# One transfer of dense expert weights for eight blocks into one buffer, in place of four blocks into each of two

## The chip, the cores and the metric

The kernel runs on one core of one Trainium2 chip. The metric is the device time of one execution in microseconds, the median of the runs. The core has five engines that run side by side and each take their instructions strictly in the order of the program: TensorE (PE; its weight loads are PEld), VectorE (DVE), ScalarE (ACT), GpSimd (POOL) and SyncE (SP, which here issues nearly all plain DMAs). The tile framework adds the semaphore waits, and its scheduler, which plays the program through against a model, fixes the order on each engine when the program is built.

## The reference, cut to what matters

An encoder layer for 1024 tokens of width 1024 ends in a PEER feed-forward: each token picks 8 x 16 of 16384 experts and sums their outputs.

```python
def chunk(xc):
    q = (xc @ w_q).reshape(C, PEER_HEADS, 2, PEER_DK // 2)
    s = jnp.einsum('chpd,hpnd->chpn', q, sub_keys)
    ...
    g = jax.nn.softmax(best, axis=-1)
    u = u_tab[eidx]
    a = jax.nn.gelu(jnp.einsum('chkd,cd->chk', u, xc), approximate=False)
    vv = v_tab[eidx]
    return jnp.einsum('chk,chkd->cd', (g * a).astype(vv.dtype), vv)
```

## The kernel before

The PEER part treats the eight tiles of 128 tokens in two ways. Three tiles (`NG`) go through `gather`: for each of 128 picks POOL fetches one row of `peer_u` or `peer_v` per token by an indirect DMA (L1249, tile `grow`), and DVE takes a dot product with it (L1262) or adds it to `gacc` (L1270). These DMAs run in a queue of POOL's own. Five tiles (`DENSE`, 640 tokens) are computed densely over all 16384 experts, in 128 blocks of 128 experts:

- `u_part(i)` (U): 48 matmuls of 320 columns give the activations `A` (128 experts x 640 tokens) of block i, with Gelu on ACT (L1221). 72 blocks (`EARLY`) are done ahead and parked in DRAM (`a_d`); the other 56 are done in the last stage.
- `build_g` has written the dense gate weights to DRAM as `g_d`, token slice by token slice: 20 slices of 32 tokens, each 128 x 128 x 32. For one block a partition's piece in one slice is 32 floats, and neighbouring blocks lie side by side.
- `weigh(i)` multiplies `A` by the block's gate weights `gt` on DVE (L1372) and splits the product into `wh` and `wl` (L291 on ACT, L292 on DVE). The first block of each four (`GI`) issues the DMA that loads `gt` for the four (L1368). `gt` has two buffers, so a load waits until the last multiply that reads the four before the last four is done.
- `v_group` (V) takes eight weighed blocks (`GRP`), in two halves of 512 columns. For each block it loads `vr` from `peer_v` (L1392, three buffers), splits it into `vh` (ACT, L291) and `vl` (DVE, L292; four buffers each), and runs 15 matmuls of 512 columns into five accumulators, which DVE then adds to `f_sb` (L1409).

The last stage consists of 16 such groups; 9 use parked blocks and 7 compute theirs. SP issues `vr`, `A`, `ur` (for U) and `gt` in one queue, in the order that the scheduler gave them: a `vr` that stands behind a `gt` is issued behind it and moves behind it. DVE mixes the work of the dense part with that of `gather`, ACT does the `vh`, `wh` and `uh` casts and the Gelu. `A` has three buffers, `wh` and `wl` eight each.

Of the kernel before, what the change touches and what calls it, by code (L numbers as in the profile page):

```python
# [10 lines left out]
F32 = mybir.dt.float32  # L11
# [10 lines left out]
P = 128  # L22
# [11 lines left out]
GRP = 8  # L34
# [255 lines left out]
def split(nc, hi, lo, src):  # L290
    nc.scalar.copy(hi, src)  # L291
    return nc.vector.tensor_sub(lo, src, hi)  # L292
# [3 lines left out]
def layer(ctx: ExitStack, tc: tile.TileContext, a: dict, out: bass.AP):  # L296
# [835 lines left out]


    CS = 32
    GI = 4
    NCS = TD // CS
    jx_d = dram.tile([NT, 3, P, P], BF16, name="jx_d")
    NB = 4
# [219 lines left out]
    ep = s_e.enter_context(tc.tile_pool(name="ep", bufs=2, side="left"))  # L1358
# [3 lines left out]
    def weigh(i, A):  # L1362
        if A is None:
            A = up.tile([P, TD], F32, name="A", bufs=3)
            nc.sync.dma_start(A, a_d[i])
        if i % GI == 0:
            gt = ep.tile([P, NCS, GI, CS], F32, name="gt")
            nc.sync.dma_start(gt, h_view[:, :, i:i + GI, :])  # L1368
            G[i // GI] = gt
        gt = G[i // GI]  # L1370
        Av = A.rearrange("p (s c) -> p s c", c=CS)
        nc.vector.tensor_mul(Av, Av, gt[:, :, i % GI])  # L1372
        wh = ep.tile([P, TD], F32R, name="wh", bufs=GRP)
        wl = ep.tile([P, TD], F32R, name="wl", bufs=GRP)
        split(nc, wh, wl, A)
        return wh, wl
# [85 lines left out]
    for n, g in enumerate(order):  # L1462
        W, As = [], {}

        def first_half(b):
            if g >= n_e:
                As[b] = u_part(g * GRP + b, u_late)
                tick(UC)

        if n == 0:  # L1470
            for b in range(3):
                first_half(b)
        with ExitStack() as s_i:
            if n == 0:
                s_i.enter_context(tc.issue_after(loads[-1].ins))
            for c in range(DENSE if n == 0 else 0):
                nc.sync.dma_start(f_sb[:, c], h2_d[NG + c])
            for b in range(GRP):
                if b not in As:
                    first_half(b)  # L1480
                W.append(weigh(g * GRP + b, As.get(b)))
            if n == n_g - 1:
                load_last_ln()
            v_group(g * GRP, W, n == 0, n == n_g - 1)
# [70 lines left out]
```

## Time and profile before

| what | value |
|---|---|
| median of 3 runs | 3265.74 us (3262.74 to 3266.41) |
| the profiled execution | 3255.75 us, its span 3254.0 us |
| PE busy over the span | 2988.5 us, 92% |
| DVE busy over the span | 2735.7 us, 84% |
| `gt` loads | 32, 1280 KB each |
| `gt` multiplies (L1372) | 128, 820 ns each |
| last stage | about 1905 us to the end |

Read the table of stretches first (which engine is full in which stage), then the waits of the engine that is full, then the order of time on SP, PE, ACT and DVE around the waits that are found. A row of the order of time has start and duration in us, the engine (a "q" marks its sequencer), the line, and in brackets the idle time before it and what ended it.

### The profile page before, as it was taken

The numbers are of one execution on the slowest core, as the hardware profiler recorded it, in microseconds if no ns is written. First come the engines' busy times: TensorE is split into PE (matmuls) and PEld (weight loads), VectorE is DVE, ScalarE is ACT, GpSimd is POOL, SyncE is SP. The second block draws the span as 40 slices with busy tenths as digits, with TensorE's granted clock in tenths as the row PEclk, the third lists the DMA queues.
The fourth block names the chain that finished last, engine by engine and source line by source line (L and its number), as shares of the span: only waits on it lengthen the run. The fifth ranks groups of instructions, "written<-read, shape, count | busy, mean of one in ns | idle before, by whom it ended". The sixth has DMA issues, their size and how long they took to land.

```text
span 3254.0 us, 44798 instructions
## 1 busy us (share of the span) xinstructions
PE 2988.5 (92%) x15582; PEld 2552.1 (78%) x15582; DVE 2735.7 (84%) x5514; ACT 1256.2 (39%) x2454; POOL 1036.4 (32%) x797
## 2 busy tenths in 40 slices
PE   6999898889999779999999789998999999799997
PEld 5677676556689778999898778886888888588886
DVE  7556799888757799999999768888889879888888
ACT  4544344455523216766574122222222222122222
POOL 0000000000000351332435735555555445455551
PEclk9999889989999989999999899999999999999998
DMA  5244743322444777887888999999999999989995
GB/s 173 97 149 133 249 123 104 102 56 73 138 152 149 278 252 241 302 303 277 310 284 319 364 338 336 325 358 341 329 358 323 353 315 333 337 302 353 342 332 188
DMA packets 355064, 828.87 MB, mean 255 GB/s; under 512 B 34345, under 2 KB 144851, under 8 KB 351253
## 3 DMA queue, kind: packets, MB, share of 16 engines
q0 software_dynamic: 110592, 402.70, 34.5%
q1 hardware_dynamic: 230709, 356.71, 33.9%
q10 hardware_dynamic: 13536, 66.59, 5.2%
q8 instruction: 123, 2.02, 0.2%
q14 instruction: 104, 0.85, 0.1%
HBM read 715.52 MB, written 110.33 MB: 254 GB/s over the span
## 4 chain that ended last, share of the span: by engine, by line
PE 31%; DVE 22%; DMA 7%; issue 6%; POOL 3%; ACT 1%; SPq 0%; DVEq 0%; POOLq 0%; ACTq 0%
PE ps_x L285 5%; PE ps_x L287 5%; PE ps_x L286 5%; DVE grow L1262 4%; DVE gacc L1270 4%; DMA vr<-in_peer_v 3%; PE ps_h L285 3%; PE ps_h L287 3%; PE ps_h L286 3%; POOL grow L1249 3%; DVE p L1160 2%; PE ps_o L285 2%; PE ps_o L286 2%; PE ps_o L287 2%; DVE ul L292 2%
## 5 line engine op out<-in xcount | busy, mean ns | idle before, releaser
L1249 POOL DMA_INDIRECT grow<-in_peer_u,eid x384 | 518.0, 1349 | 582.3 <-DVE grow L1262 206.9
L1249 POOL DMA_INDIRECT grow<-in_peer_v,eid x384 | 504.8, 1315 | 606.1 <-DVE gacc L1270 267.3
L1270 DVE SCALAR_TENSOR_TENSOR gacc<-grow,dot,gacc 128x1024 f32<-128x1024 f32 x381 | 487.3, 1279 | 13.2 <-DMA grow<-in_peer_v,eid 9.6
L1262 DVE SCALAR_TENSOR_TENSOR grow<-grow,gh 128x1024 f32<-128x1024 f32 x384 | 460.1, 1218 | 19.8 <-DMA grow<-in_peer_u,eid 19.5
L287 PE MATMUL ps_x<-hd,ul 128*128 128x320 f32 x1152 | 368.3, 328 | 50.1 <-DVE ul L292 49.7
L285 PE MATMUL ps_x<-hd,uh 128*128 128x320 f32 x1152 | 373.6, 325 | 28.4 <-ACT uh L291 26.2
L286 PE MATMUL ps_x<-hd,uh 128*128 128x320 f32 x1152 | 370.3, 322 | 0.0
L286 PE MATMUL ps_x<-vl,wh 128*128 128x512 f32 x864 | 341.1, 395 | 1.7 <-DVE vl L292 1.6
L287 PE MATMUL ps_x<-vh,wl 128*128 128x512 f32 x864 | 336.8, 393 | 0.0
L285 PE MATMUL ps_x<-vh,wh 128*128 128x512 f32 x864 | 302.3, 396 | 28.4 <-ACT vh L291 23.2
L291 ACT CAST vh<-vr 128x512 fp32r<-128x512 f32 x256 | 156.3, 619 | 388.4 <-DMA vr<-in_peer_v 280.6
L285 PE MATMUL ps_h<-hd,uh 128*128 128x320 f32 x896 | 278.8, 311 | 9.0 <-ACT A L1221 5.6
L286 PE MATMUL ps_h<-hd,uh 128*128 128x320 f32 x896 | 278.3, 311 | 0.0
L287 PE MATMUL ps_h<-hd,ul 128*128 128x320 f32 x896 | 275.8, 311 | 2.5 <-DVE ul L292 2.5
L287 PEld LDWEIGHTS ps_x<-hd,ul 128*128 128x128 f32 x1152 | 222.7, 195 | 65.0 <-DVE ul L292 59.0
L285 PEld LDWEIGHTS ps_x<-hd,uh 128*128 128x128 f32 x1152 | 225.9, 196 | 35.4 <-ACT uh L291 31.8
L292 DVE TENSOR_TENSOR vl<-vr,vh 128x512 fp32r<-128x512 f32 x256 | 174.5, 687 | 75.7 <-ACT vh L291 74.4
L286 PEld LDWEIGHTS ps_x<-hd,uh 128*128 128x128 f32 x1152 | 225.8, 196 | 0.8
L291 ACT CAST uh<-ur 128x1024 fp32r<-128x1024 f32 x128 | 134.7, 1052 | 223.7 <-DMA ur<-in_peer_uT 103.1
L285 PEld LDWEIGHTS ps_x<-vh,wh 128*128 128x128 f32 x864 | 162.7, 190 | 63.5 <-ACT vh L291 24.7
L292 DVE TENSOR_TENSOR ul<-ur,uh 128x1024 fp32r<-128x1024 f32 x128 | 155.5, 1215 | 63.8 <-ACT uh L291 62.4
L286 PEld LDWEIGHTS ps_x<-vl,wh 128*128 128x128 f32 x864 | 164.4, 190 | 37.1 <-DVE vl L292 4.4
(366 smaller groups left out, 6876.3 us busy)
## 6 DMA issues: line engine op xcount, KB each, us to landing
ur<-in_peer_uT SPq DMA_DIRECT2D x128, 512.0 KB
vr<-in_peer_v SPq DMA_DIRECT2D x256, 256.0 KB
g_d<-gst ACTq DMA_DIRECT2D x20, 2048.0 KB
gt<-g_d SPq DMA_DIRECT2D x32, 1280.0 KB
a_d<-A ACTq DMA_DIRECT2D x72, 320.0 KB
A<-a_d SPq DMA_DIRECT2D x72, 320.0 KB
fw<-in_dft_fw SPq DMA_DIRECT2D x64, 256.0 KB
wr<-in_w_in SPq DMA_DIRECT2D x16, 512.0 KB
```

The lines of the kernel that those rows point to most:

```text
L285: nc.tensor.matmul(out, L[0], R[0], start=start, stop=False)
L286: nc.tensor.matmul(out, L[0], R[1], start=False, stop=False)
L287: return nc.tensor.matmul(out, L[1], R[0], start=False, stop=stop)
L291: nc.scalar.copy(hi, src)
L292: return nc.vector.tensor_sub(lo, src, hi)
L1160: nc.vector.tensor_tensor(p1, iota.unsqueeze(1).to_broadcast([P, NB, P]), ig[:, 0, c:c + NB].unsqueeze(2).to_broadcast([P, NB, P]), op=ALU ...
L1249: nc_i = nc.gpsimd.indirect_dma_start(out=t, out_offset=None, in_=a["peer_" + kind], in_offset=bass.IndirectOffsetOnAxis(ap=eid[g][:, k:k ...
L1262: nc.vector.scalar_tensor_tensor(t, t, 1.0, h_t, op0=ALU.mult, op1=ALU.mult, accum_out=d[:, k - k0:k - k0 + 1])
L1270: nc.vector.scalar_tensor_tensor(acc, t, dots[k0][:, k - k0:k - k0 + 1], acc, op0=ALU.mult, op1=ALU.add)
```

## The change

`GI` becomes `GRP`, 8, and `gt` gets one buffer in place of two. A `gt` tile then holds eight blocks (128 partitions x 20 slices x 8 blocks x 32 tokens, 20 KB a partition) where it held four (10 KB); the room taken is the same. There are 16 loads of 2560 KB where there were 32 of 1280 KB. Each is made of 2560 runs, now of 1024 bytes, before of 512. The load of a group now waits for the eighth multiply of the group before it.

```diff
-    GI = 4
+    GI = GRP
...
-            gt = ep.tile([P, NCS, GI, CS], F32, name="gt")
+            gt = ep.tile([P, NCS, GI, CS], F32, name="gt", bufs=1)
             nc.sync.dma_start(gt, h_view[:, :, i:i + GI, :])
```

How the order moves is shown at the eleventh group of the last stage. SP's queue before, from the load for the first half of the twelfth group to the one for its second half (`vr` blocks of V, `A` parked activations, `ur` rows for U):

```order
L1368 DMA gt_25256<-g_d_7559 128x20x128
L1392 DMA vr_24849<-in_peer_v 128x512
L1365 DMA A_24806<-a_d_7563 128x640
L1392 DMA vr_24878<-in_peer_v 128x512
L1365 DMA A_24813<-a_d_7563 128x640
L1392 DMA vr_24905<-in_peer_v 128x512
L1365 DMA A_25254<-a_d_7563 128x640
L1202 DMA ur_25902<-in_peer_uT 128x1024
L1392 DMA vr_24929<-in_peer_v 128x512
L1365 DMA A_25263<-a_d_7563 128x640
L1392 DMA vr_24956<-in_peer_v 128x512
L1368 DMA gt_25286<-g_d_7559 128x20x128
```

SP's queue now, at the same place in the program:

```order
L1392 DMA vr_24856<-in_peer_v 128x512
L1365 DMA A_25232<-a_d_7563 128x640
L1392 DMA vr_24883<-in_peer_v 128x512
L1392 DMA vr_24907<-in_peer_v 128x512
L1365 DMA A_25241<-a_d_7563 128x640
L1368 DMA gt_25234<-g_d_7559 128x20x256
L1392 DMA vr_24934<-in_peer_v 128x512
L1365 DMA A_25248<-a_d_7563 128x640
L1392 DMA vr_24958<-in_peer_v 128x512
```

The earlier of the two loads is gone, and the one that is left stands where the later one stood, with twice the columns and `vr` loads right behind it.

DVE before, from the eighth multiply of the eleventh group (`A_24813`) to the first multiply of the twelfth (`A_25254`):

```order
L1372 TENSOR_TENSOR A_24813<-A_24813,gt_24792 128x640
L1266 TENSOR_TENSOR dot_24536<-dot_24536,gat2_6485 128x16
L1270 SCALAR_TENSOR_TENSOR gacc_23152<-grow_24725,dot_24536,gacc_23152 128x1024
L292 TENSOR_TENSOR wl_24817<-A_24813,wh_24816 128x640
L292 TENSOR_TENSOR vl_24908<-vr_24905,vh_24907 128x512
L1270 SCALAR_TENSOR_TENSOR gacc_23152<-grow_24749,dot_24536,gacc_23152 128x1024
L1372 TENSOR_TENSOR A_25254<-A_25254,gt_25256 128x640
```

DVE now, from the eighth multiply of the eleventh group (`A_24791`, whose end releases the load) to the first of the twelfth (`A_25232`, which waits for that load):

```order
L1372 TENSOR_TENSOR A_24791<-A_24791,gt_24742 128x640
L292 TENSOR_TENSOR vl_24859<-vr_24856,vh_24858 128x512
L1270 SCALAR_TENSOR_TENSOR gacc_23136<-grow_24848,dot_24516,gacc_23136 128x1024
L292 TENSOR_TENSOR wl_24795<-A_24791,wh_24794 128x640
L1270 SCALAR_TENSOR_TENSOR gacc_23136<-grow_24853,dot_24516,gacc_23136 128x1024
L1270 SCALAR_TENSOR_TENSOR gacc_23136<-grow_24877,dot_24516,gacc_23136 128x1024
L292 TENSOR_TENSOR vl_24886<-vr_24883,vh_24885 128x512
L1270 SCALAR_TENSOR_TENSOR gacc_23136<-grow_24880,dot_24516,gacc_23136 128x1024
L292 TENSOR_TENSOR vl_24910<-vr_24907,vh_24909 128x512
L1270 SCALAR_TENSOR_TENSOR gacc_23136<-grow_24904,dot_24516,gacc_23136 128x1024
L1270 SCALAR_TENSOR_TENSOR gacc_23136<-grow_24928,dot_24516,gacc_23136 128x1024
L1372 TENSOR_TENSOR A_25232<-A_25232,gt_25234 128x640
```

The next group's first multiply has moved from five instructions behind the eighth to ten behind it. Over the 15 places of this kind ten to sixteen instructions stand between. The scheduler also gave the stages before the last one another order in places, with the same instructions.

## Rows read from the trace of the kernel before

**Rows 1.** The page, its first line.

```profile
span 3254.0 us, 44798 instructions
```

**Rows 2.** Stretches: length, busy time and instructions by engine, granted clock, DMA share, GB/s.

```profile
core 0: us, PE busy (x) PEld busy (x) DVE busy (x) ACT busy (x) POOL busy (x), PEclk, DMA share, GB/s
...
0.00:1905.00 1905.00, 1707.21 (x9124) 1438.84 (x9125) 1584.40 (x3954) 904.07 (x1872) 358.23 (x289) 0.95 0.60 204
...
1905.00:3190.00 1285.00, 1233.93 (x6252) 1074.42 (x6252) 1100.70 (x1485) 335.71 (x556) 672.28 (x505) 0.98 0.95 335
...
1905.00:3254.00 1349.00, 1281.28 (x6460) 1113.22 (x6459) 1151.31 (x1560) 352.10 (x582) 678.20 (x508) 0.98 0.93 326
```

**Rows 3.** Waits in 1905 to 3254: who, for whom, total us, times, longest.

```profile
PE ps_x L285 <- ACT vh L291: 23.2, 4, 10.0
PE ps_o L285 <- ACT vh L291: 14.5, 4, 5.7
...
ACT vh L291 <- DMA vr<-in_peer_v: 280.6, 83, 16.9
...
DVE A L1372 <- DMA gt<-g_d: 11.2, 2, 9.9
```

**Rows 4.** The page's DMA issues (KB each), and the tile gt.

```profile
gt<-g_d SPq DMA_DIRECT2D x32, 1280.0 KB
...
L1372 DVE TENSOR_TENSOR A<-A,gt x128: 808/820/829, 1925.3 to 3191.3; 128x640 f32<-128x640 f32 x128
```

**Rows 5.** Order of time: one load after a fourth multiply, four stalls behind such.

```profile
2827.06 0.38 SPq L1368 DMA_DIRECT2D gt<-g_d  x1
2828.80 12.30 SPq L1392 DMA_DIRECT2D vr<-in_peer_v  x1
...
2849.16 1.22 PE L285 MATMUL ps_x<-vh,wh 128*128 128x512 f32 x2 [10.00 <-ACT vh L291]
...
2265.17 0.74 PE L285 MATMUL ps_o<-vh,wh 128*128 128x512 f32 x2 [3.12 <-ACT vh L291]
...
2774.85 0.73 PE L285 MATMUL ps_o<-vh,wh 128*128 128x512 f32 x2 [4.18 <-ACT vh L291]
...
2682.66 0.41 PE L285 MATMUL ps_h<-hd,uh 128*128 128x320 f32 x1 [3.10 <-ACT A L1221]
```

**Rows 6.** Order of time: a load after an eighth multiply, two stalls behind such.

```profile
2203.25 0.38 SPq L1368 DMA_DIRECT2D gt<-g_d  x1
...
2225.05 1.22 PE L285 MATMUL ps_x<-vh,wh 128*128 128x512 f32 x2 [7.01 <-ACT vh L291]
...
2800.15 1.22 PE L285 MATMUL ps_o<-vh,wh 128*128 128x512 f32 x2 [5.69 <-ACT vh L291]
```

**Rows 7.** Order of time: first and last of 15 loads after an eighth multiply.

```profile
1992.30 0.37 SPq L1368 DMA_DIRECT2D gt<-g_d  x1
...
2014.38 0.69 DVE L292 TENSOR_TENSOR vl<-vr,vh 128x512 fp32r<-128x512 f32 x1
...
2019.27 0.39 PE L285 MATMUL ps_o<-vh,wh 128*128 128x512 f32 x1
...
3136.15 0.37 SPq L1368 DMA_DIRECT2D gt<-g_d  x1
...
3156.64 0.69 DVE L292 TENSOR_TENSOR vl<-vr,vh 128x512 fp32r<-128x512 f32 x1 [1.76 <-ACT vh L291]
...
3158.00 0.84 PE L285 MATMUL ps_x<-vh,wh 128*128 128x512 f32 x3
```

**Rows 8.** Chain of waits: a vr ahead of any gt, start, us, what.

```profile
2198.90 5.87 DMA vr<-in_peer_v
```

**Rows 9.** Stretches: two gt loads almost alone; one beside the gathers.

```profile
1919.00:1929.00 10.00, 6.34 (x44) 6.08 (x42) 3.69 (x6) 2.74 (x5) 0.00 (x0) 1.00 1.17 303
...
2831.00:2847.00 16.00, 8.16 (x35) 6.12 (x33) 11.38 (x19) 1.98 (x3) 5.11 (x5) 0.90 1.06 378
```

**Rows 10.** Groups of instructions in 1905 to 3254: busy us, mean ns, idle before.

```profile
L1270 DVE SCALAR_TENSOR_TENSOR gacc<-grow,dot,gacc 128x1024 f32<-128x1024 f32 x254 | 325.5, 1281 | 6.7 <-DMA grow<-in_peer_v,eid 3.9
...
L292 DVE TENSOR_TENSOR vl<-vr,vh 128x512 fp32r<-128x512 f32 x256 | 174.5, 687 | 75.7 <-ACT vh L291 74.4
```

## The prediction

> **What bounds the kernel now.** I read the table of stretches first. All that the change touches lies in the last stage, from 1905 us on: there PE is busy for 1281 of 1349 us and for 1234 of the 1285 us before the tail [rows 2]. PE bounds this stage; DVE, with 1151 us, has 198 us to spare. So an added PE stall goes onto the end one for one, and only what takes a PE stall away is a gain. The DMA share is 0.95 at 335 GB/s [rows 2]: the queues are full too, and who stands behind whom in them matters.
>
> The second view is PE's waits. Eight of them, 37.7 us together, are for `vh`, the cast of a block of `peer_v` on ACT, and ACT in turn waits 280.6 us for the transfer of `vr` [rows 3]. The multiply that reads `gt` hardly ever waits for it: 11.2 us in two waits, 9.9 of them at the stage's start [rows 3]. So `gt` is not late for its own reader, and a view of that reader alone would call the load free.
>
> The third view is the order of time around PE's stalls. Every long one behind the start stands behind a `gt` load. At 2827.06 a `gt` is issued; the `vr` issued next holds SP for 12.30 us, and PE stands for 10.00 us until 2849.16 [rows 5]. The load is a plug in SP's queue, and what it delays is `vr`. Of the 32 loads two open the stage, 15 are released by the fourth multiply of a group (first kind) and 15 by the eighth (second kind). Behind loads of the first kind PE stands 10.00, 3.12, 4.18 and, by way of the Gelu queued behind a late `vh` on ACT, 3.10 us: 20.4 us [rows 5]. Behind two of the second kind it stands 7.01 and 5.69 us [rows 6].
>
> **The change part by part.** The work on the engines stays as it is: 128 multiplies of 820 ns [rows 4], the same casts, the same matmuls. Sixteen issues of some 0.37 us leave SP, which isn't the bound; I cost that at nothing.
>
> *The first-kind loads go.* Their 20.4 us of stalls go with them: -20.4. What is late next is the load that is left.
>
> *The second-kind loads double.* Two quantities decide. One is the margin that `vr` has today. For the first of the 15 the `vl` of the next `vr` ends at 2015.07 and its first product starts at 2019.27, a margin of 4.2 us; for the last the two are 3157.33 and 3158.00, 0.7 us [rows 7]. Thirteen of the 15 have a margin, about 2.5 us in the mean (the mean of these two is 2.4); the other two are the stalls of rows 6 and have none. PE gets through this because it holds some 20 us of work when the load is issued, and the `vr` behind the load needs about 20 us: 22.8 for the first, 21.2 for the last [rows 7], 16.5 to 23.3 over the 15, 19.9 in the mean. It is balanced to within 3 us, by the order that the scheduler laid.
>
> The other quantity, X, is how much later that `vr` comes. Of the 19.9 us, 5.9 are those of a `vr` with no `gt` ahead [rows 8] and about 2 are the two splits with their hand-over; so 12 us are the load's. Its bytes double. What a byte costs in runs of 512 bytes is seen where two loads move almost alone: 303 GB/s at a share of 1.17 is 259 GB/s for full engines, against 335 at 0.95, or 353, over the stage [rows 2, 9], that is 1.36 times the stage's cost. Runs of 1024 bytes lie between. If they cost as the stage's mean does, the load takes 2 / 1.36 = 1.47 times as long, and X is 0.47 x 12 = 5.6 us. Half way, at 1.18, it takes 1.74 times as long, and X is 8.9. If a byte gets no cheaper, X is 12. Below 5.6 speaks nothing but the way in which the queues share the engines (a rival). I take 7.3, the middle of 5.6 and 8.9, since beside the gathers the whole already moves 378 GB/s with `gt` in it [rows 9], so the short runs cost less there than alone.
>
> Each of the 15 loads then costs PE X less its margin: 15 x 7.3 - 13 x 2.5 = 109.5 - 32.5 = 77 us more than now. The later `vr` loads in that queue come late by no more than the first; their lateness is the same stall, not a new one.
>
> *The weights come later themselves.* Until now the next group's first multiply followed the eighth within some 4 us, its `gt` long there; now it waits for a load issued only then, about 12 x 1.6 + 3 = 22 us. `wh` and `wl` of a group are ready 20 to 40 us ahead of their first product in most groups, because their slots come free one by one during the last V half; so I cost this at nothing on PE. If that cover were gone, it would add to the same 15 places. On DVE it is a wait in order: between the two multiplies stand about ten instructions, six of 1.28 and three of 0.69 us among them [rows 10], some 11 us, so that DVE stands about 11 us in each place, 165 us in all, with gathers, `vl` and `f_sb` queued behind. It has 198 us idle in the stage [rows 2] and these are partly the same stretches, in which it now waits for late `vh`. I cost it at nothing and price it below.
>
> *The start.* Before, both halves of the first group's load stood ahead of the first `vr`, as the whole does now: 0. *The earlier stages* get another order of the same work. PE is idle there for 198 of 1905 us [rows 2]; I take 0, and 10 us either way, a twentieth of that.
>
> **The sum.** -20.4 + 77 = +57 us. Against the profiled execution: span 3254.0 [rows 1] + 57 = 3311 us, and 3313 with the 1.75 us around it. That execution lies 10 us below the median of the runs shown; on that median, 3265.74, the forecast is 3323 us.
>
> **The rivals.** *(a) The long load fits under PE's cover* (faster). This decides if X is below the margin, 2.5 us. Then only the 20.4 us go: 3245 us. For it: 378 GB/s with a `gt` in flight against 335 over the stage [rows 2, 9]. Against it: bytes double, and the cheapest byte in sight gives 5.6.
>
> *(b) The queues share by descriptors* (about no change). If POOL's and SP's queues take turns by a count of runs, SP's queue moves more bytes a turn with longer runs. With the load at about a third of the engines' time now, its turn grows by 1.74 and the others' stays, so the load takes 0.33 x 1.74 + 0.67 = 1.24 times as long, X is 2.9, and the sum 15 x 2.9 - 32.5 - 20.4 = -9 us: 3257 us. For it: the high rate of the stretch with `gt` in flight; against it: the margins are so thin that one late load in three undoes the gain. The Trainium skill states such a rule (DMA: Bandwidth & Descriptors, "Queues, rings and completion order": each engine goes round the rows that have work and drains a whole packet of some descriptors before it switches). No row here splits the engines' time by queue, so the trace neither bears it out nor denies it; by that rule alone the time would be the 3257 us above, and by the rows' price per byte it is 3323.
>
> *(c) DVE's wait comes on top* (slower still). If the 165 us in which DVE stands in order fall where it is not idle today, `vl` comes late after the load too and PE stalls twice. The point is where standing and the present 1151 us fill the stage: 1316 of 1349, so about half of the added waits would show. That gives 57 + 80 = +137, or 3403 us. A full doubling (X of 12: 180 - 53 = +127, 3393 us) lands beside it.
>
> *(d) The change does not do what it says.* The order rules this out: the loads are 16, of 256 columns.
>
> **How the numbers follow.** The forecast (X of 5 to 11, +22 to +112) gets 0.62, (c) with the full doubling 0.14, (b) 0.12, (a) 0.12. A measurement of this kernel tells about 0.2% from no change, 6.5 us. (b) puts its chance half into no change and half into faster, with a little of the forecast's low end in no change: faster 0.16, same 0.09, slower 0.75. The range reaches from 3268, which leaves out (a) and most of (b), to 3385, which takes in X up to about 11.5 and leaves out the worse part of (c).
>
> **What would show it.** In the profile after, PE's waits for `vh` should grow from 37.7 to about 110 us, in some 13 to 15 stalls of 4 to 15 us, each behind one of the 16 loads; the `vr` behind a load should be split about 27 us after the load's issue. The multiply's wait for `gt` should go from 11 us to 100 us or more on DVE. The stage's DMA share should fall a little, as 42 MB move in longer runs. If the `vr` behind a load comes after some 23 us, the price per byte is wrong and (a) or (b) holds; if PE waits for `vl` or `wh` rather than for `vh`, it is (c); if the stage keeps its length and the earlier ones don't, the reordering decides.

## The result, and the profile after

The kernel after takes 3295.81 us (median of 4, 3289.93 to 3299.64), the kernel before beside it 3264.24 us (4 runs, 3262.41 to 3266.41): a ratio of 1.009, interval 1.0075 to 1.0104, +32 us. The forecast was slower, by 57 us; the loss is a little over half of that. The profiled execution after is 3289.93 us, its span 3288.1.

The stretches of the kernel after (columns as in [rows 2]):

```profile
0.00:1905.00 1905.00, 1707.51 (x9112) 1440.00 (x9113) 1584.13 (x3952) 903.26 (x1871) 358.62 (x289) 0.95 0.60 203
...
1905.00:3289.00 1384.00, 1294.04 (x6472) 1118.14 (x6470) 1150.58 (x1563) 353.74 (x583) 687.87 (x508) 0.97 0.90 319
```

Up to 1905 us nothing changed (PE 1707.21 before [rows 2]): the whole loss lies in the last stage, 1384 us for 1349. DVE works as long as before, 1151 us; the DMA share fell from 0.93 to 0.90. The waits of the stage in the kernel after (who, for whom, total us, times, longest), which answer to [rows 3]:

```profile
ACT vh L291 <- DMA vr<-in_peer_v: 294.6, 75, 21.9
...
DVE A L1372 <- DMA gt<-g_d: 128.5, 16, 13.1
...
PE ps_o L285 <- ACT vh L291: 22.9, 6, 14.0
...
PE ps_x L285 <- ACT vh L291: 21.5, 5, 12.4
...
PE ps_o L286 <- DVE vl L292: 7.5, 6, 2.4
...
PE ps_x L286 <- DVE vl L292: 6.2, 6, 1.6
```

The multiply now stands for its `gt` 16 times, 128.5 us against 11.2. PE's waits for `vh` grew only from 37.7 to 44.4 us, and waits for `vl`, on DVE, stand beside them with 13.7. The two largest `vh` stalls are those of [rows 6]. The first of them in the order of time after (start, us, engine; in brackets the idle time before and its releaser):

```profile
2214.72 0.38 SPq L1368 DMA_DIRECT2D gt<-g_d  x1
...
2216.60 13.88 SPq L1365 DMA_DIRECT2D A<-a_d  x1
...
2223.04 1.07 PE L285 MATMUL ps_x<-vh,wh 128*128 128x512 f32 x4
...
2230.57 0.40 SPq L1392 DMA_DIRECT2D vr<-in_peer_v  x1
...
2237.19 0.82 DVE L1372 TENSOR_TENSOR A<-A,gt 128x640 f32<-128x640 f32 x1 [11.70 <-DMA gt<-g_d]
...
2238.69 0.62 ACT L291 CAST vh<-vr 128x512 fp32r<-128x512 f32 x1 [18.88 <-DMA vr<-in_peer_v]
...
2239.36 2.07 PE L285 MATMUL ps_x<-vh,wh 128*128 128x512 f32 x4 [12.45 <-ACT vh L291]
2239.86 0.68 DVE L292 TENSOR_TENSOR vl<-vr,vh 128x512 fp32r<-128x512 f32 x1
```

This is the plug of the prediction: behind the load SP is held 13.88 us by the next issue, the `vr` goes out 15.9 us after the load, and PE stands 12.45 us where it stood 7.01. DVE stands too, but its wait ends at 2237.19, 1.5 us ahead of the `vh`: both wait for the same queue, one behind the other. So it is behind all 15 second-kind loads: the stand ends before that `vh` starts, and of the 128.5 us in which DVE stands 87 lie within ACT's waits for `vr`, 31 within PE's idle time. The second large stall is alike:

```profile
2803.25 0.38 SPq L1368 DMA_DIRECT2D gt<-g_d  x1
...
2826.30 1.56 DVE L1372 TENSOR_TENSOR A<-A,gt 128x640 f32<-128x640 f32 x2 [10.09 <-DMA gt<-g_d]
2826.96 0.62 ACT L291 CAST vh<-vr 128x512 fp32r<-128x512 f32 x1 [21.89 <-DMA vr<-in_peer_v]
2827.63 1.22 PE L285 MATMUL ps_o<-vh,wh 128*128 128x512 f32 x2 [14.03 <-ACT vh L291]
```

These two make 26.5 of the 44.4 us; in both, a group of parked blocks follows a group of parked blocks, and PE holds only 10 to 11 us of work when the load is issued.

**A book of PE's time.** For every kernel I took the starts of the matmuls from the first to the last product of V. The distance to the next start is 227 ns for a product of V and 147 ns for one of U when PE runs freely; 3839 and 2496 of them make 1238.4 us. What is over is a gap (over 0.3 us), a matmul of about twice the time (half clock), or small change. I also took, for each load, the time from its issue to the end of the `vh` and of the `vl` of the next `vr` ("vh after load", "vl after load").

| us | before | after | change |
|---|---|---|---|
| V, first to last product | 1305.9 | 1338.2 | +32.3 |
| gaps within 32 us of a first-kind load | 24.6 | 0 | -24.6 |
| gaps within 32 us of a second-kind load | 17.7 | 52.9 | +35.2 |
| gaps elsewhere (of these for `vl`) | 7.8 (1.3) | 23.4 (13.8) | +15.6 |
| matmuls at half clock | 13.0 | 16.2 | +3.2 |
| small | 4.5 | 7.2 | +2.7 |
| vh after a second-kind load, mean of 15 | 18.8 | 23.2 | +4.4 |
| vl after a second-kind load, mean of 15 | 19.9 | 25.5 | +5.6 |
| load, issue to last packet, mean of 15 | 15.1 | 21.0 | +5.9 |

### The profile page after: what moved, and what is told of

It is laid out like the page before. It is cut to its first block, busy times and chain, and to the rows that moved or that the text cites. A ratio compares the mean times of both kernels' runs of the same rounds, so it can differ in the third digit from the quotient of the medians.

```text
span 3288.1 us, 44825 instructions
## 1 busy us (share of the span) xinstructions
PE 3001.6 (91%) x15582; PEld 2558.1 (78%) x15582; DVE 2734.7 (83%) x5514; ACT 1257.0 (38%) x2454; POOL 1046.5 (32%) x797
## 5 line engine op out<-in xcount | busy, mean ns | idle before, releaser
L1249 POOL DMA_INDIRECT grow<-in_peer_u,eid x384 | 530.0, 1380 | 583.0 <-DVE grow L1262 179.3
L1262 DVE SCALAR_TENSOR_TENSOR grow<-grow,gh 128x1024 f32<-128x1024 f32 x384 | 460.6, 1216 | 26.2 <-DMA grow<-in_peer_u,eid 25.9
L1372 DVE TENSOR_TENSOR A<-A,gt 128x640 f32<-128x640 f32 x128 | 103.8, 819 | 141.0 <-DMA gt<-g_d 128.5
```

Of the source, the lines that this page charges most:

```text
L1249: nc_i = nc.gpsimd.indirect_dma_start(out=t, out_offset=None, in_=a["peer_" + kind], in_offset=bass.IndirectOffsetOnAxis(ap=eid[g][:, k:k ...
L1262: nc.vector.scalar_tensor_tensor(t, t, 1.0, h_t, op0=ALU.mult, op1=ALU.mult, accum_out=d[:, k - k0:k - k0 + 1])
```

## The experiments: first, what was compared

The kernels beside which my runs were timed were the kernel before, built anew, and they took not 3264 but 3293 to 3297 us, in the last comparison 3312. I had the shown kernels built and timed anew, without an edit.

> The kernel before once more, for a profile on the chip of the runs beside it: ratio 1.000 within 0.003. P and D both: PE's stalls for vh behind loads come again, 35 to 50 us in all, PE's waits for vl under 5 us.

Measured: 3296.89 us, 1.0002 of the kernel before as built beside it (0.9984 to 1.0019), some 32 us above the time that stood in front of the prediction.

> The changed kernel once more, on the chip of the runs beside it: ratio to the kernel before 1.006 to 1.012. The load lands 20 to 22 us after its issue, DVE stands 120 to 140 us for it, PE waits some 45 us for vh and 10 to 18 us for vl.

Measured: 3297.09 us, 0.9997 (0.9983 to 1.0011). The loss that I expected between the two isn't there.

The traces tell why: the same source had become another order of instructions. On SP, where the loads can be followed by name, three orders occur: one (both kernels of the first comparison), two (c_after), three (c_before). The cause is line 215, in the helper that lays out a network of additions in an early stage. It gives buffers back in the order of a Python set, which changes from build to build; another buffer gives other waits, and the scheduler lays everything behind it anew. With a fixed order in that line, before and after have the same order on SP up to the last stage; the differences in the earlier stages that the prediction speaks of were this, and not the change. The edits, for order one and for order three:

```diff
-        for q in {a, b}:
+        for q in dict.fromkeys((a, b)):
```

```diff
-        for q in {a, b}:
+        for q in sorted({a, b}, key=lambda q: zlib.crc32(repr((4, q)).encode())):
```

> The kernel before with one line of a helper of the early stages fixed: run_net gives back the buffers of an operation's two operands in the order of a Python set, which differs from build to build; here first operand first. The order on SP is then that of the kernel before's profiled build (order one). Theory N (which of a few orders a build falls into moves the time by 1%, the chip doesn't): 3259 to 3270 us, about 0.990 of the kernel before as it is built beside this run, if that is the build of some 3296 us. Rival (the two chips differ by 1%): 3290 to 3300 us, ratio 1.000.

Measured: 3264.68 us, 0.9898 of the kernel before beside it (0.9871 to 0.9926).

> The changed kernel with the same line fixed in the same way: the same order as the run beside it up to the last stage, so that the difference is the change alone. N, and the plug with DVE's standing as read from the two profiles: 3291 to 3301 us, 1.008 to 1.011 of the run with order one. If the 32 us came with the chip or with the earlier stages: within 6 us of that run.

Measured: 3294.96 us, 1.0003 (0.9988 to 1.0019). In order one the change costs 30.3 us, so the +32 are the change's, and not a difference between the orders of two builds.

> The kernel before with the order of those buffers drawn by a fixed rule that gives the order on SP of the other profiled build of the kernel before (order three). N: 3290 to 3303 us, 26 to 38 us above order one on this chip, some 10 us of it before the last stage. Rival (chips): equal to order one.

Measured: 3293.32 us, 0.9997 (0.9981 to 1.0014).

> The changed kernel by the same rule as order three. If the change costs 32 us in any order: 3322 to 3335 us. If its price is the margin that order one happened to have (in the profile of order three PE stands 71 us in gaps, where order one has 50 and the changed kernel 76): 3294 to 3306 us, within 8 us of order three before the change.

Measured: 3290.94 us, 0.9987 (0.9969 to 1.0004). In order three the change costs nothing, since the kernel before is already as slow. PE's longest kinds of waits in the stage, d_before_three and then d_before_one:

```profile
PE ps_x L285 <- ACT vh L291: 27.3, 9, 9.3
...
PE ps_o L285 <- ACT vh L291: 17.0, 6, 8.5
...
PE ps_x L286 <- DVE vl L292: 8.8, 4, 3.0
...
PE ps_o L286 <- DVE vl L292: 4.6, 5, 2.0
```

```profile
PE ps_x L285 <- ACT vh L291: 25.8, 6, 10.0
...
PE ps_o L285 <- ACT vh L291: 12.9, 5, 7.5
...
PE ps_x L286 <- DVE vl L292: 2.2, 4, 1.0
...
PE ps_o L286 <- DVE vl L292: 1.5, 2, 1.3
```

The load and its landing are the same in both (15.6 to 15.9 us); what differs is the margin between the `vl` behind a second-kind load and PE's first product on it: 1.9 to 2.2 us in the mean in order one (5 or 6 of 15 at 1 us or less), 1.2 to 1.3 in order three (8 or 9 of 15), -1.0 to -1.6 in all kernels after. So V's book in order three reads 1335.2 us before and 1334.0 after, where order one has 1309.8 and 1335.3. What the change takes away is in part the margin that order one happened to have: of the 25 us between the two orders before, 12 are gaps behind second-kind loads, 3 other gaps and some 10 matmuls at half clock. Why order three has more of these the runs don't show.

## The experiments: the plug, or VectorE standing

Two causes come with one edit: the load is twice as long (theory P: what counts is the plug in SP's queue), and with a single buffer it is issued so late that DVE stands (theory D). Since orders differ, each kernel is named with its order; the runs e2 to e5 were made before I had found this. Ratios are to the kernel before as built beside each run; on that scale order one has 0.9898 before and 1.0003 after. Which order that kernel had when it took 3312 us isn't known; so for the four runs beside it (names with f) V's book is given too.

**The load off SP's queue.** Four blocks, two buffers, order three:

```diff
-            nc.sync.dma_start(gt, h_view[:, :, i:i + GI, :])
+            nc.scalar.dma_start(gt, h_view[:, :, i:i + GI, :])
```

> The kernel before with the 32 gt loads issued on ACT's DMA queue in place of SP's; two buffers of four blocks, same bytes. P: no vr stands behind a load any more, and the 42 us of PE stalls behind loads go: 3215 to 3235 us. Rival (the 16 DMA engines are full, so vr is late whoever stands in which queue): 3255 to 3270 us. If ACT, which now waits in order to issue a load, holds up its casts: slower than 3270 us, with PE waits for vh that no landing explains.

Measured: 3262.40 us, 0.9902 (0.9875 to 0.993). The time lies in the range of the rival (full DMA engines), but that range took the kernel before for 3264 us; beside the 3293 of order three it is a gain of some 31. In that order, with little margin, taking the plug out of SP's queue gives back what was lost: PE's waits for `vh` fall from 44.3 to 10.7 us, while those for `vl` rise from 13.4 to 22.5. The same edit in order one:

> The kernel before with its loads of four blocks, two buffers, issued from ScalarE's queue instead of SP's, in order one. No load stands ahead of a gather's transfer on SP any more, and VectorE stands no more than before. Theory P: SP's queue is where the load costs, and TensorE's waits of about 50 us in the stage shrink: 3235 to 3258 us. Theory M (order one has so much margin that the load of four blocks costs nothing there): 3262 to 3268 us, as the kernel before in order one (3264.7). In order three the same edit took 3262.4 against 3295, 33 us less.

Measured: 3283.80 us beside 3312.27 of the kernel before, which ran 0.5% slower in that comparison than in the others, 0.9921 (0.9893 to 0.9948): no gain on order one's 0.9898. V takes 1314.2 us, with 3.5 us more of U in it, against 1309.8. PE's waits have moved, not gone:

```profile
DVE A L1372 <- DMA gt<-g_d: 44.6, 7, 9.1
...
PE ps_o L286 <- DVE vl L292: 18.6, 7, 5.5
...
PE ps_x L286 <- DVE vl L292: 9.5, 5, 5.3
...
PE ps_o L285 <- ACT vh L291: 5.2, 1, 5.2
...
PE ps_x L285 <- ACT vh L291: 5.0, 4, 2.4
```

The time lies above both ranges of the expectation. So off SP's queue the load gains nothing where the margin is there: 3262.40 us in order three, 3264.68 in order one without the edit. Now the load of the kernel after on ACT's queue (`GI = GRP`, `bufs=1`, `nc.scalar` in the load), order one:

> The changed kernel with its 16 loads on ACT's queue: still one buffer, DVE still stands for each load. P alone: the 53 us of PE stalls within 32 us of a load go: about 3245 us. D alone: DVE stands as long as in the changed kernel, 110 to 150 us, and the time stays at 3285 us or more. Both, as the stalls of the changed kernel divide (53 us behind loads, 21 us elsewhere): 3245 to 3262 us, PE's waits for vl still 10 us or more.

Measured: 3359.73 us, 1.020 (1.0161 to 1.0239), the miss that corrected me most:

```profile
DVE A L1372 <- DMA gt<-g_d: 178.8, 15, 15.4
...
PE ps_x L286 <- DVE vl L292: 42.0, 12, 11.6
PE ps_o L286 <- DVE vl L292: 39.5, 10, 15.5
...
PE ps_o L285 <- ACT vh L291: 11.1, 5, 5.9
...
PE ps_x L285 <- ACT vh L291: 4.0, 2, 3.6
```

No `gt` stands ahead of a `vr` any more, and PE waits 81.5 us for `vl`, which is queued on DVE behind the multiply that stands: 11.9 us in the mean. No issue of SP is held for over 2 us in the last stage, where the kernel after has 17 such. V takes 1401.1 us. The load lands 25.0 us after its issue here, against 21.0 on SP, so the stands are longer than in the kernel after. Standing alone, at that length, can cost more than the whole change.

**Standing at the old length.** Four blocks in a load, one buffer, in order two and, with line 215 fixed, in order one:

```diff
-            gt = ep.tile([P, NCS, GI, CS], F32, name="gt")
+            gt = ep.tile([P, NCS, GI, CS], F32, name="gt", bufs=1)
```

> Four blocks a load as in the kernel before, but one gt buffer: 32 loads of 1280 KB, each issued only when the multiply that frees the buffer is done, each used right after. Theory P (a vr that stands behind a load in SP's queue is what costs): the loads are as long and as many as before, so within 20 us of the kernel before, 3245 to 3285 us. Theory D (DVE stands in its order for a load that is issued only then, and vl and the gathers behind it come late): DVE stands about 31 times some 5 to 8 us, more than the 128 us of the changed kernel, and the time is 3290 us or more; PE's waits for vl grow past the 14 us of the changed kernel.

Measured: 3352.05 us, 1.0173 (1.0137 to 1.0209).

> Four blocks in a load as before, but one buffer instead of two, and the helper's loop in a fixed order (order one, whose kernel before took 3264.7 us and whose kernel after took 3295.0). The load is as short as before, so the gathers' transfers behind it in SP's queue are no later for its length; only VectorE's standing at the single buffer is left, at 29 loads instead of 15. Theory P (nearly all of the 30 us is the longer transfer that stands ahead of the gathers' transfers): 3265 to 3280 us. Theory D (VectorE's standing carries a large share of it): VectorE waits over 120 us for the tile of gate weights, TensorE's waits grow by over 40 us, 3310 us or more, since the same edit in order two took 3352.

Measured: 3348.23 us, 1.0133 (1.0088 to 1.0178); against order one's 0.9898 that is +2.4%, some 78 us (V: 1386.0 against 1309.8). DVE and PE in f_four_one:

```profile
DVE A L1372 <- DMA gt<-g_d: 149.6, 26, 10.0
...
PE ps_x L285 <- ACT vh L291: 54.6, 11, 11.9
...
PE ps_o L285 <- ACT vh L291: 27.5, 7, 8.3
```

Theory P, as I put it, falls: the load is no longer than before (it lands after 16.9 us, before 15.7), and PE loses far more. But D isn't the whole either: the waits are for `vh`, that is for `vr`, not for `vl`. Per load after the first, the time from its issue to the first product on the block behind it exceeds PE's work in between by 3.7 us (31 loads), against 3.4 in the kernel after (15 loads) and 1.8 in the kernel before in order one (30 loads): with one buffer a load costs about the same at either length. The `vh` behind it ends 22.9 us after its issue, nearly as late as in the kernel after (23.2), though the load lands 4 us earlier. By what way the stand makes the next `vr` late, these runs don't show.

**Two transfers for a buffer.** The buffer of eight blocks filled by two loads of four, one behind the other, order one:

```diff
-            nc.sync.dma_start(gt, h_view[:, :, i:i + GI, :])
+            for k in range(0, GI, 4):
+                nc.sync.dma_start(gt[:, :, k:k + 4], h_view[:, :, i + k:i + k + 4, :])
```

> The changed kernel's one buffer of eight blocks, filled by two transfers of four blocks each (runs of 512 bytes again), issued one behind the other. The first multiplies need the first transfer alone. P: the vr behind the pair comes as late as behind one load or some 3 us later, 15 places: as slow as the changed kernel or up to 40 us slower, ratio to the kernel before 1.009 to 1.022. D: the wait of the first multiply falls from 22 to some 13 us after the issue, DVE stands under 50 us in all, and the ratio falls to 0.998 to 1.004.

Measured: 3308.14 us, 1.0032 (1.0014 to 1.0051), some 10 us more than the kernel after in order one on the same scale, though the two intervals just touch. V takes 1357.1 us against 1335.3, but the execution traced here lies 5 us above its median and the one there 9 below.

```profile
DVE A L1373 <- DMA gt<-g_d: 91.0, 14, 10.2
...
PE ps_x L285 <- ACT vh L291: 28.8, 7, 10.8
PE ps_o L285 <- ACT vh L291: 28.2, 7, 14.0
```

DVE stands 37 us less, since the first half is there earlier, and PE waits 13 us more for `vh`; the `vl` behind the pair ends 26.2 us after its issue in the mean, against 25.5. Less standing did not help here. The plug is a little longer with runs of 512 bytes; that it makes the whole difference is a reading that fits, and not shown.

**Half the bytes.** Ten of the twenty token slices are loaded and each is used twice; the gate weights of half of the dense tokens are left out of the computation. One buffer, order three and order one; and two buffers, order one. The edit with two buffers (`GI = GRP` in all three; with one buffer, `bufs=1` is added):

```diff
-            gt = ep.tile([P, NCS, GI, CS], F32, name="gt")
-            nc.sync.dma_start(gt, h_view[:, :, i:i + GI, :])
+            gt = ep.tile([P, NCS // 2, GI, CS], F32, name="gt")
+            nc.sync.dma_start(gt, h_view[:, 0:NCS // 2, i:i + GI, :])
...
-        Av = A.rearrange("p (s c) -> p s c", c=CS)
-        nc.vector.tensor_mul(Av, Av, gt[:, :, i % GI])
+        Av = A.rearrange("p (h s c) -> p h s c", h=2, c=CS)
+        half = gt[:, :, i % GI].unsqueeze(1).to_broadcast([P, 2, NCS // 2, CS])
+        nc.vector.tensor_mul(Av, Av, half)
```

> The changed kernel with ten of the twenty token slices loaded and each used for both halves of the tokens (the gate weights of half of the dense tokens are left out): 16 loads of 1280 KB in runs of 1024 bytes, one buffer, release and use as in the changed kernel. P: a load lands some 11 to 12 us after its issue, the vr behind it is split after some 16 us, below the 20 us of work that PE holds; no stall over 2 us behind a load is left: 3220 to 3240 us. D: DVE stands only 1 to 3 us a load, so this too falls away: the same 3220 to 3240. If instead the scheduler's other order makes the 32 us of the change, it stays at 3285 to 3300.

Measured: 3221.96 us, 0.9777 (0.9749 to 0.9805), order three, where before and after stand at 0.9997 and 0.9987.

> As the run with half the bytes (ten of twenty token slices loaded, each used twice), but with two buffers of eight blocks, so that a load is issued a whole group ahead and DVE has nothing to stand for. Loads as long as there. D: the 43 us in which DVE stood there cost PE something even at this length: ratio to the kernel before 0.965 to 0.973. P alone: the plug is as long, 0.975 to 0.981 as with one buffer.

Measured: 3217.03 us, 0.9749 (0.9729 to 0.9768).

> Eight blocks in a load and one buffer, but only ten of the twenty token slices are loaded and each is used twice, so the gate weights of half of the dense tokens are left out of the computation. The load has 1280 KB as the kernel before, in 512-byte... runs of 1024 bytes as the kernel after. Order one. Beside the run with the same half load in two buffers (3217.0 us), which stands nowhere, it shows what one buffer's standing costs alone. Theory P: 3217 to 3223 us. Theory D: VectorE waits 40 us or more for the tile and the time is 3228 us or more.

Measured: 3231.20 us, 0.9763 (0.9731 to 0.9796). Its waits, and then those of e8_half_two:

```profile
DVE A L1373 <- DMA gt<-g_d: 40.8, 13, 9.2
...
PE ps_o L286 <- DVE vl L292: 5.5, 5, 2.2
...
PE ps_o L285 <- ACT vh L291: 3.8, 1, 3.8
PE ps_x L285 <- ACT vh L291: 3.5, 1, 3.5
```

```profile
DVE A L1373 <- DMA gt<-g_d: 10.4, 1, 10.4
...
PE ps_o L286 <- DVE vl L292: 5.3, 3, 3.1
...
PE ps_x L285 <- ACT vh L291: 3.9, 1, 3.9
...
PE ps_o L285 <- ACT vh L291: 3.1, 2, 1.8
```

V takes 1265.5 us with one buffer and 1264.6 with two. So stands of some 2.6 us in each of twelve places (40.8 less the 9.2 of the longest) cost V nothing in these two traces: there is cover for short ones. By the medians it is less sure. They lie 14 us apart, in theory D's range, by the ratios 0.1%, within the noise; a price of a few us isn't excluded. With a load that lands after 13 us, instead of 21, PE's waits for `vh` all but vanish.

**The long plug without the standing.** The half load in two buffers, and right behind it on SP's queue a copy of the other ten slices to a scratch array that nobody reads; order one:

```diff
-            nc.sync.dma_start(gt, h_view[:, 0:NCS // 2, i:i + GI, :])
+            ld = nc.sync.dma_start(gt, h_view[:, 0:NCS // 2, i:i + GI, :])
+            with tc.issue_after(ld.ins):
+                nc.sync.dma_start(waste[i // GI], h_view[:, NCS // 2:, i:i + GI, :])
```

> The same half load (ten of twenty token slices, each used twice; the gate weights of half of the dense tokens are left out) in two buffers, and right behind it on SP's queue a copy of the other ten slices to a scratch array that nobody reads, so that the queue is held for as long as by the kernel after's load, or longer, while VectorE has its tile early. Order one. Without the copy: 3217.0 us. Theory P: the gathers' transfers behind the copy land as late as in the kernel after or later, TensorE's waits return, 3280 us or more. Theory D: without VectorE's standing the stage goes as without the copy, 3217 to 3235 us. Between the two, the distance says which share of the loss is the transfer's length; the copy writes as much as it reads, so what it costs is an upper bound for the length.

Measured: 3289.89 us, 0.9929 (0.9905 to 0.9952), 1.8% above the same kernel without the copy, which is some 59 us; V grows by as much, from 1264.6 to 1323.9 us.

```profile
PE ps_x L285 <- ACT vh L291: 21.4, 6, 9.0
...
PE ps_o L285 <- ACT vh L291: 17.9, 5, 9.8
...
PE ps_o L286 <- DVE vl L292: 9.0, 6, 3.1
DVE A L1376 <- DMA gt<-g_d: 9.0, 1, 9.0
...
PE ps_x L286 <- DVE vl L292: 7.0, 6, 3.0
```

DVE stands once, at the start, and yet PE's waits are nearly those of the kernel after: 39.3 us for `vh` (44.4), 16.0 for `vl` (13.7). The vl after a load comes after 23.8 us (17.9 without the copy, 25.5 in the kernel after), and from issue to first product PE loses 48.1 us over the 15 loads after the first (13.6 without, 51.0 in the kernel after). The 59 us are the price of the other half of the bytes, not of the change. Beside the kernel before in order one, which reads the same bytes in twice as many loads, V is 14 us longer (1309.8), beside the kernel after 11 us shorter (1335.3); by the ratios 0.3% and 0.7%. This is no clean bound for the length: the copy writes what it reads, which costs, while the `vh` behind it ends 22.7 us after the load's issue, half a microsecond sooner than in the kernel after.

**What follows.** Each cause alone costs time, measured by V against the kernel before in order one: the long plug without standing (f_long_two) 14 us, the standing without a plug (e5) 91 and the standing at the old length (f_four_one) 76; in the last two DVE stands for longer than in the kernel after. In that kernel both are there, and a large part of the standing lies where `vr` is late anyway (87 of 128.5 us). As far as f_long_two goes, about half of the 25 us of V is the plug's and half DVE's. How the 30 us would split if one could be taken away with everything else kept stays open: a second buffer of 20 KB a partition would show it, and that was not tried.

## Why the prediction was right or wrong

**Right: the place, the direction and the plug.** The loss lies in the last stage, the earlier ones kept their time (+0.3 us of PE's 1707), and the longest stalls are for `vh`, behind a `gt` that plugs SP. The first-kind stalls went as forecast: -24.6 us by the book, against the -20.4 of four rows. DVE's wait for `gt` is 128.5 us, where 100 or more was forecast.

**Wrong, in one line:** the step that failed is the second-kind term, 15 x 7.3 - 32.5 = +77 us; the gaps behind those loads grew by 35.2, and PE's waits for `vh`, forecast at about 110 us, are 44.4. Beside it the standing of DVE, put at nothing on PE, came to +15.6.

**Wrong: X.** I took 7.3 us; it is 5.6, from 19.9 to 25.5, the forecast's own lower bound. Of that the plug makes 4.4, by which the `vh` comes later; the other 1.2 come on DVE, where the `vl` follows its `vh` later than before. Queue q1, which carries `gt`, shows what a byte costs (packets, MB, share of the 16 engines' time). Before:

```profile
q1 hardware_dynamic: 230709, 356.71, 33.9%
```

After:

```profile
q1 hardware_dynamic: 189493, 356.71, 32.7%
```

The same bytes took 27.9 us less of the 16 engines' time (0.339 x 3254.0 - 0.327 x 3288.1), nearly all of it the `gt` loads': by their own packets it is 25.9, as a run took 50 ns at 1024 bytes and 30 at 512, so a byte costs 0.83 of before. That is dearer than the 0.735 from which I had the 5.6; by 0.83, two times the bytes are 1.67 times the engines' time, but the load lands only 1.39 times as late (21.0 against 15.1). From its first packet to its last it takes 18.4 us against 12.5, 1.48 times as long, which is the 1.47 of the lower bound, come about in another way.

The packets of the 15 loads show how. While a load moved, its packets held 0.39 of the engines' time before and 0.43 after, and 1.67 x 0.39 / 0.43 is 1.5. What gave way is the rest of SP's own queue (0.14 and 0.09); POOL's queue with the gathers kept 0.52 and 0.50. This goes against rival (b): by turns of a fixed count of runs, SP's queue would have gained on POOL's as its runs grew longer, but its share was 0.53 before and 0.52 after.

**Wrong: the loss per place.** Fifteen times X less the margin would be 51.5 us even with X at 5.6; the gaps behind the second-kind loads grew by 35.2. The two places of [rows 6] went about as forecast, 7.01 to 12.45 and 5.69 to 14.03. The thirteen others together lose 21 us more than before (35.2 less the 13.8 of these two), 1.6 each, where I had 4.8 each and X at 5.6 would give 3.1. I measured the margin from the end of `vl` to the first product on the block; but PE begins a block with the products of `vh` alone, and at 2239.36 it started 1.2 us before the `vl` ended (2239.86 and 0.68). That part of the margin I left out. Measured to the end of `vh` the 15 margins before are 3.3 us in the mean, to the end of `vl` 2.2, so it accounts for about 1.1 of the 1.5 us by which 3.1 is too large.

**Wrong: "the weights come later" at nothing.** PE does not wait for `wh` (4.8 us once), there the cover held. But the multiply that stands holds up `vl` and `f_sb` behind it on DVE: +15.6 us of gaps elsewhere, most of them for `vl`. Rival (c) had this mechanism and priced it at 80, by a share of DVE's idle time in the whole stage. Two thirds of the standing lie where ACT waits for the late `vr` anyway, and in the traces of f_half_one and e8_half_two short stands cost V nothing; e5 shows what standing costs without a plug beside it. The rule against this part is one that the Trainium skill gives in a line (Trainium Kernel Development and Optimization, "Best Practices": double-buffer, to overlap DMA with compute), and f_four_one bears it out with 78 us.

**The sum as measured:** -24.6 + 35.2 + 15.6 + 3.2 + 2.7 = +32. That the prediction's own sum with X at 5.6 gives +31 is chance in part: one term too large by 16, another too small by 16.

**What I had not considered:** that the kernel before was one of several orders of the same source. The +32 holds for the order that was shown; in order three the answer is nothing (0.9987 against 0.9997). The forecast's margins were read from one order, and of the two orders tried in both kernels its direction holds for that one alone.

## What to carry to other kernels

The price of a longer transfer is paid first by whoever stands behind it in its queue, even where its reader never waited; look at the next transfers' margins before making it longer, and measure a margin to the first instruction that truly needs the late tile. Giving up the second buffer ties the issue to the last reader, and an in-order engine then stands with all that is queued behind it; here stands of some 2.6 us were covered, stands of 6 to 12 us in the mean were not. Before two builds of a scheduled kernel are compared, make the build reproducible: a loop over a set, far from the change, moved the time by nearly as much as the change did (28.6 and 30.3 us).

## What the runs showed of the hardware

An issue on SP behind a long load can be held: 13.88 us for the `A` at 2216.60, 15.1 us at most. In the kernel after 17 of SP's issues in the last stage took over 2 us, all within 12 us after a load was issued. Before that stage none did, nor with the load on ACT's queue (e5, f_act_queue). So the plug blocks transfers that are not even issued yet.

The same 2560 KB landed after 25.0 us from ACT's queue and after 21.0 from SP's. Between SP's queue and POOL's, the engines' time stayed divided about in halves when SP's runs went from 512 to 1024 bytes (0.53 and 0.52 before, 0.52 and 0.50 after).

And a long stall is paid twice. In the 12.45 us without work the granted clock of TensorE fell from 1.00 to 0.50, the lower of its two levels; the four products at 2239.36 then took 2.07 us, where four such took 1.07 before it. Over the stage 16.2 us went that way, 13.0 before.
